# Router on rows ahead of their norm, and a top-k sorted in parts during the output projection

## The chip, the core and the metric

One core of one Trainium2 chip runs the whole program in one launch. The metric is device time in microseconds (us); less is better. Every time below comes from the recorded runs or from the profile of one execution.

## The reference, cut to what matters

One encoder layer on 1024 tokens of width 1024: an input norm and projection, three mixers (retention, S5, windowed attention), an output projection with a residual and a layer norm, and then sixteen SwiGLU experts, each of which takes the 128 tokens with the highest softmax affinity for it.

```
h   = LN(alpha*h + concat(retention, S5, attention) @ W_out)      # g = ln1_g, b = ln1_b
aff = softmax(h @ router_w)                                       # 1024 tokens x 16 experts
gates, idx = top_k(aff.T, 128)                                    # 128 tokens for each expert
xs  = h[idx]
out = (silu(xs @ w_gate) * (xs @ w_up)) @ w_down * gates          # for each expert
h   = LN(alpha*h + scatter_add(out))
```

## The kernel before

Tokens come in eight tiles of 128 rows (`NT`). The program has two halves.

**The mixers and the output projection.** A loop over `i` works in half tiles. A step computes the attention scores of one (tile, head group) pair, the attention output of the pair one step earlier (`attention_out`: DVE multiplies four score tiles by 1/sum in L790, PE transposes them into `tp`, ACT and DVE split them into a high and a low float32r part, PE multiplies with V), and one half of the output projection of a tile three steps behind that (`out_proj_half`, 24 matmuls of 512 columns, then `z = ALPHA*z + mm` on DVE, L838). After the second half, `out_proj_norm` does the layer norm (statistics on DVE, the power on POOL, L62 and L63 on DVE), stores the rows to `h1_dram` and ALPHA times the rows to `acc_dram`. Five steps later `router` transposes the normed rows, multiplies by `router_w` (L866, `rw` stationary, 128 columns moving), turns the 16 x 128 result back (L868, L870) and takes the softmax into `K.aff`. In this half a planner orders the instructions of each engine, from the order of the program, dependencies and its own cost estimates.

**The top-k.** `top_k` runs after all eight tiles: one transpose of the 128 x 128 affinities, eight rounds of maximum-of-8 and replace on two 64-column halves (L931, L934), bitonic merges (`bitonic`: two DVE instructions per stage, L886 and L887) on 128, 64 and 32 rows, a last merge over PE, the threshold `tau` (L956), masks, counting matmuls (L968 to L975) and `K.slot` (L984). `expert_hot`, `expert_slots` and `expert_gather` turn `slot` into token numbers; an indirect DMA on POOL gathers 128 rows of `h1_dram` (L1014).

**The experts.** 384 pieces of weights of 1 MB each pass through PE, 12 matmuls of 512 columns apiece. This half is ordered by hand on all engines. For each piece SP loads `wraw` (L1069), ACT copies the high part into `whl` (L71), DVE subtracts for the low part (L72). Eight raw buffers hold the first eight loads: two in pool `raw` (never closed), three in `raw2` (right end of the on-chip memory), three in `raw0`. Six `whl` buffers of 16 KB lie in `hl2` (left end). `Experts.start` issues the eight loads, six cuts (`cut` = high and low part; for pieces 0 to 2, `POOL_FIRST`, the low part is POOL's), and the first gather. The pools of the second half are opened where pools of the first half were closed, and the first use of a pool waits for all accesses of the closed pools whose bytes it takes: before, `raw2` lies over `hl` (which holds `rt`), `hl2` over `hy` (the output weights), `ast` and a part of `op` (the output projection's tiles).

Of the kernel before, what the change touches and what calls it, by code (L numbers as in the profile page):

```python
# [36 lines left out]
POOL_FIRST = 3  # L37
# [742 lines left out]
def attention_out(K, i):  # L780
# [8 lines left out]
    for g in range(4):  # L789
        nc.vector.tensor_scalar(S[g][:, :W], S[g][:, :W], rd[:, g:g + 1], None, op0=OP.mult)  # L790
# [28 lines left out]
def out_proj_load(K, t):  # L819
    nc, pool = K.nc, K.op  # L820
    y = pool.tile([P, 4, P], F32, name="y", bufs=2)
    nc.sync.dma_start(y, K.y_dram[t])
    z = pool.tile([P, D], F32, name="z", bufs=3)
    nc.sync.dma_start(z, K.h_dram[t])
    yh = pool.tile([P, KC, P], F32R, name="yh", bufs=3)
    yl = pool.tile([P, KC, P], F32R, name="yl", bufs=3)
    split(K, yh[:, 0:4, :], yl[:, 0:4, :], y)
    K.Y[t] = yh, yl, z


def out_proj_half(K, t, n):
# [6 lines left out]
    nc.vector.scalar_tensor_tensor(z[:, ns], z[:, ns], ALPHA, ps, op0=OP.mult, op1=OP.add)  # L838


def out_proj_norm(K, t):
    nc, pool = K.nc, K.op
    z = K.Y[t][2]
    layer_norm_tile(K, pool, z, z, K.g1, K.b1, "l1")
    nc.sync.dma_start(K.h1_dram[t * P:(t + 1) * P, :], z)
    K.rt[t] = K.hl.tile([P, 2, D], F32, name="rt", tag="whl")
    ah = K.rt[t][:, 0, :]
    nc.scalar.activation(ah, z, AF.Copy, scale=ALPHA)
    nc.sync.dma_start(K.acc_dram[t * P:(t + 1) * P, :], ah)


def router(K, t):
    nc, pool = K.nc, K.op
    z = K.Y.pop(t)[2]
    hT = K.rt.pop(t)[:, 1, :].rearrange("p (c f) -> p c f", c=KC)
# [11 lines left out]
    lT = pool.tile([E, P], F32, name="lT", bufs=2)  # L867
    nc.vector.tensor_copy(lT, pr[0:E, :])  # L868
    pl = K.psm.tile([P, E], F32, name="sm")
    nc.tensor.transpose(pl, lT, K.ident[0:E, 0:E])  # L870
    s = pool.tile([P, 4], F32, name="rsm", bufs=2)
    a = pool.tile([P, E], F32, name="aff", bufs=2)
    nc.vector.tensor_reduce(s[:, 0:1], pl, AX.X, OP.max)
    nc.vector.tensor_scalar(s[:, 1:2], s[:, 0:1], -1.0, None, op0=OP.mult)
    nc.scalar.activation(a, pl, AF.Exp, bias=s[:, 1:2], accum_out=s[:, 2:3])
    nc.vector.reciprocal(s[:, 3:4], s[:, 2:3])
    nc.vector.tensor_scalar(K.aff[:, t, :], a, s[:, 3:4], None, op0=OP.mult)


def bitonic(K, pool, x, rows, k, name):  # L880

    nc = K.nc
    while k:
        y = pool.tile([rows, P], F32, name=name, bufs=2)
# [24 lines left out]

def top_k(K):  # L910
# [4 lines left out]
    nc = K.nc  # L915
    aff = K.aff.rearrange("p t e -> p (t e)")
    with K.tc.tile_pool(name="topk", bufs=1, side="left") as pool:
        pt = K.ptp.tile([P, 4, P], F32, name="tp")
        nc.tensor.transpose(pt[:, 0, :], aff, K.ident)
        rest = [K.aff] + [pool.tile([P, NT, E], F32, name=f"rest{i}") for i in range(2)]  # L920
        for i in range(3):
            nc.gpsimd.tensor_copy(K.tok[:, :, :, 2 + i], rest[i])
            if i < 2:
                nc.gpsimd.tensor_tensor(rest[i + 1], rest[i], K.tok[:, :, :, 2 + i], OP.subtract)
        w = [[pool.tile([P, 64], F32, name=f"w{h}{i}") for i in range(2)] for h in range(2)]
        half = [pool.tile([P, 64], F32, name=f"half{h}") for h in range(2)]
        for h in range(2):
            nc.vector.tensor_copy(w[h][0], pt[:, 0, h * 64:(h + 1) * 64])
        for i in range(8):
            for h in range(2):  # L930
# [596 lines left out]
```

## Time and profile before

| what | value |
|---|---|
| median of three runs | 1745.15 us (1738.24, 1745.15, 1745.46) |
| the profiled execution's own time | 1739.56 us |
| its span, first to last instruction | 1737.9 us |
| busy: PE, DVE, ACT, POOL | 1608.6, 1435.3, 1058.7, 335.5 us |
| mean granted TensorE clock | 0.968 of full speed |
| read and written in the memory off chip | 465.01 MB, 46.14 MB |

The span is cut into stages by the lines that run in them. Busy time of an engine is a mean over stages with different limits, so the views of single stretches in the section on rows say more than this table.

### The profile page before, as it was taken

Reading aid. Unit: us, or ns where it says so; the run is one execution under the profiler, and the core shown is the slowest. Engines: PE = TensorE matmul, PEld = TensorE weight load, DVE = VectorE, ACT = ScalarE, POOL = GpSimd, SP = SyncE. Lnnn points to the kernel's source line nnn. Section 1 sums busy time; section 2 is a strip of 40 time slices with the busy share of each in tenths; the row PEclk is TensorE's granted clock in tenths of the full one; section 3 lists DMA queues with packets and bytes.
Section 4 is the critical chain, followed back from the end, with each engine's and each line's share of the span. In section 5 each row is a group of like instructions: output and inputs, shape, how many; then the busy total and the mean of one; then the engine's idle time right before and its main releaser. Section 6 shows DMA issues by size and latency. Waiting matters only on the chain.

```text
span 1737.9 us, 21027 instructions
## 1 busy us (share of the span) xinstructions
PE 1608.6 (93%) x7673; PEld 1294.0 (74%) x7673; DVE 1435.3 (83%) x1678; ACT 1058.7 (61%) x1082; POOL 335.5 (19%) x403
## 2 busy tenths in 40 slices
PE   6898996899993599999999999999999999999996
PEld 4688875577772488888888888888888778778785
DVE  8687962678867688888888889888898999989995
ACT  3332331455543377777777777777777777777772
POOL 6926801001003101011010010110101213121121
PEclk9999898999997699999999999999999999999998
DMA  6353189652225399999999999999999999999993
GB/s 246 115 143 102 51 244 267 196 176 74 77 105 242 113 337 370 371 387 356 382 377 370 383 362 376 382 371 383 366 372 409 384 396 412 382 406 376 394 402 138
DMA packets 110871, 512.53 MB, mean 295 GB/s; under 512 B 12336, under 2 KB 35120, under 8 KB 60080
## 3 DMA queue, kind: packets, MB, share of 16 engines
q1 hardware_dynamic: 100640, 481.31, 73.1%
q0 software_dynamic: 10128, 29.89, 5.6%
q8 instruction: 60, 0.98, 0.2%
q14 instruction: 43, 0.35, 0.1%
HBM read 465.01 MB, written 46.14 MB: 294 GB/s over the span
## 4 chain that ended last, share of the span: by engine, by line
PE 58%; DVE 14%; DMA 12%; issue 7%; ACT 4%; POOL 3%; SPq 1%; POOLq 0%; DVEq 0%; ACTq 0%
PE gu L1038 28%; PE y L1038 13%; DVE whl L72 5%; DMA zz<-acc_d 4%; PE mm L80 3%; PE mm L82 3%; PE mm L81 3%; ACT whl L71 2%; DMA wraw<-in_exp_w_down 2%; DMA wraw<-in_exp_w_up 2%; PE tp L1023 2%; PE tp L796 1%; PE sm L866 1%; PE po L81 1%; PE po L82 1%
## 5 line engine op out<-in xcount | busy, mean ns | idle before, releaser
L72 DVE TENSOR_TENSOR whl<-wraw,whl 128x2048 fp32r<-128x2048 f32 (+1 forms) x395 | 887.0, 2256 | 136.2 <-ACT whl L71 135.8
L71 ACT ACTIVATE whl<-wraw 128x2048 fp32r<-128x2048 f32 (+1 forms) x400 | 753.3, 1887 | 260.3 <-PE gu L1038 124.1
L1038 PE MATMUL gu<-whl,xT 128*128 128x512 f32 x3072 | 748.5, 400 | 0.0
L1038 PEld LDWEIGHTS gu<-whl,xT 128*128 128x128 f32 x3072 | 573.1, 189 | 130.7 <-ACT xT L71 0.3
L1038 PE MATMUL y<-whl,hT 128*128 128x512 f32 x1536 | 369.0, 396 | 0.7 <-ACT hT L71 0.7
L1038 PEld LDWEIGHTS y<-whl,hT 128*128 128x128 f32 x1536 | 288.6, 188 | 70.6 <-ACT hT L71 0.9
L1014 POOL DMA_INDIRECT xs<-h_d,index x16 | 44.8, 2798 | 755.9 <-issue 492.7
L80 PE MATMUL mm<-hT,whl 128*128 128x512 f32 x160 | 63.6, 398 | 6.2 <-DVE qst L75 5.3
L82 PE MATMUL mm<-hT,whl 128*128 128x512 f32 x160 | 63.1, 394 | 0.0
L81 PE MATMUL mm<-hT,whl 128*128 128x512 f32 x160 | 63.0, 393 | 0.0
L71 ACT ACTIVATE hT<-tp 128x512 fp32r<-128x512 f32 x80 | 46.4, 585 | 24.5 <-PE tp L141 15.4
L72 DVE TENSOR_TENSOR hT<-tp,hT 128x512 fp32r<-128x512 f32 x80 | 54.2, 681 | 7.1 <-ACT hT L71 7.1
L80 PE MATMUL mm<-WO,yh 128*128 128x512 f32 x128 | 51.2, 400 | 2.7 <-ACT yh L71 2.7
L80 PE MATMUL mm<-whl,hT 128*128 128x512 f32 (+1 forms) x128 | 47.3, 371 | 4.2 <-ACT gate L326 1.8
L81 PE MATMUL mm<-WO,yh 128*128 128x512 f32 x128 | 50.4, 393 | 0.0
L82 PE MATMUL mm<-WO,yl 128*128 128x512 f32 x128 | 50.1, 398 | 0.0
L1023 PE MATMUL tp<-ident,hid 128*128 128x128 f32 x256 | 38.8, 274 | 9.2 <-DVE hid L1122 9.1
L1023 PEld LDWEIGHTS tp<-ident,hid 128*128 128x128 f32 x256 | 31.2, 140 | 20.4 <-DVE hid L1122 12.6
L82 PE MATMUL mm<-whl,hT 128*128 128x512 f32 (+1 forms) x128 | 46.3, 363 | 0.0
L81 PE MATMUL mm<-whl,hT 128*128 128x512 f32 (+1 forms) x128 | 46.3, 364 | 0.0
L776 ACT ACTIVATE S<-S,asm 128x384 f32<-128x384 f32 (+1 forms) x64 | 36.9, 579 | 12.5 <-DVE asm L772 12.4
L1122 DVE TENSOR_TENSOR hid<-hid,gu 128x512 f32<-128x512 f32 x64 | 43.5, 679 | 0.0
(386 smaller groups left out, 1832.1 us busy)
## 6 DMA issues: line engine op xcount, KB each, us to landing
wraw<-in_exp_w_gate SPq DMA_DIRECT2D x128, 1024.0 KB, 7.4
wraw<-in_exp_w_up SPq DMA_DIRECT2D x128, 1024.0 KB, 7.2
wraw<-in_exp_w_down SPq DMA_DIRECT2D x128, 1024.0 KB, 8.0
wraw<-in_w_in SPq DMA_DIRECT2D x8, 1024.0 KB, 6.3
x<-in_x SPq DMA_DIRECT2D x8, 512.0 KB, 5.0
h_d<-x SPq DMA_DIRECT2D x8, 512.0 KB, 2.9
wraw<-in_w_out SPq DMA_DIRECT2D x4, 1024.0 KB, 5.7
q_d<-qst SPq DMA_DIRECT2D x64, 64.0 KB, 3.6
```

Source lines behind the costliest of these rows:

```text
L71: nc.scalar.activation(hi, src, AF.Copy)
L72: eng.tensor_tensor(lo, src, hi.bitcast(F32), OP.subtract)
L80: nc.tensor.matmul(ps, a[0], b[0], start=start, stop=False)
L81: nc.tensor.matmul(ps, a[0], b[1], start=False, stop=False)
L82: nc.tensor.matmul(ps, a[1], b[0], start=False, stop=stop)
L776: nc.scalar.activation(S[g][:, :W], S[g][:, :W], AF.Exp, bias=nm[:, g:g + 1], accum_out=rs[:, g:g + 1])
L796: nc.tensor.transpose(pt[:, g, :], S[g][:, (b - b0) * P:(b - b0 + 1) * P], K.ident)
L866: nc.tensor.matmul(pr[0:E, :], K.rw[:, c, :], hT[:, c, :], start=(c == 0), stop=(c == KC - 1))
L1014: nc.gpsimd.indirect_dma_start(out=xs, out_offset=None, in_=K.h1_dram, in_offset=bass.IndirectOffsetOnAxis(ap=K.index[:, e:e + 1], axis=0))
L1023: K.nc.tensor.transpose(pt[:, c, :], src[:, (c0 + c) * P:(c0 + c + 1) * P], K.ident)
L1038: nc.tensor.matmul(ps, a[s][c], u[:, t, i * w:(i + 1) * w], start=first and id(ps) not in began, stop=last and left[id(ps)] == 0)
L1122: at(self.after, q, 3, lambda: nc.vector.tensor_tensor(self.h[q], self.h[q], self.pg[q][1], OP.mult))
```

## The change

What it does, in the order of the program:

- `attention_out`: the four multiplications by 1/sum go from DVE to ACT. The buffers `yh` and `yl` go from three to two.
- The layer norm's gain g is multiplied into the router's weights once (`router_weights`; column sums of g*w and b*w by matmuls with ones). `router` transposes the rows `z` before they are normed; `affinities` corrects with mean, 1/deviation and the two sums. The product is now tokens x experts (`hT` stationary, 16 columns moving), so that the turning back is gone.
- `out_proj_norm` is cut into `out_proj_stats`, `out_proj_gain` and `out_proj_shift`. The lag from projection to router goes from five steps to one.
- The top-k is a generator run in chunks: tiles 0 to 3 are sorted while the projection goes on, then tiles 4 and 5 are merged in; tiles 6 and 7 remain for the end. For the last two tiles DVE's order is written by hand.
- Temporary tiles of the sort live in a pool `tk` on the left, between `ast` and `op`; those after the threshold in a pool `tks`, opened on the right after `hl` is closed and closed before `raw2` is opened.
- The count of tokens above the threshold is added by eight more matmuls of 128 columns; three DVE instructions form `slot` where eight did.
- In `Experts`, `cut` is split into `high` and `low`. `start` issues all six high parts, the gather, low parts 0 to 2 on DVE (not POOL), the first token tiles, then low parts 3 to 5. The gather is issued before the gate values are formed.

The diff, cut to its core:

```diff
@@ attention_out, out_proj_load
-        nc.vector.tensor_scalar(S[g][:, :W], S[g][:, :W], rd[:, g:g + 1], None, op0=OP.mult)
+        nc.scalar.activation(S[g][:, :W], S[g][:, :W], AF.Copy, scale=rd[:, g:g + 1])
-    yh = pool.tile([P, KC, P], F32R, name="yh", bufs=3)
+    yh = pool.tile([P, KC, P], F32R, name="yh", bufs=2)
@@ out_proj_half
+    nc.vector.bn_stats(K.st[t][:, n, :], z[:, ns])
@@ router
-    pr = K.psm.tile([P, P], F32, name="sm")
+    pr = K.psm.tile([P, E], F32, name="sm")
     for c in range(KC):
-        nc.tensor.matmul(pr[0:E, :], K.rw[:, c, :], hT[:, c, :], start=(c == 0), stop=(c == KC - 1))
+        nc.tensor.matmul(pr, hT[:, c, :], K.rw[:, 0, c, :], start=(c == 0), stop=(c == KC - 1))
...
+def affinities(K, t):
+    nc.vector.scalar_tensor_tensor(nl[:, 0], K.rsum[:, 0], mean, pr, op0=OP.mult, op1=OP.subtract)
+    nc.vector.scalar_tensor_tensor(nl[:, 1], nl[:, 0], rs, K.rsum[:, 1], op0=OP.mult, op1=OP.subtract)
+    nc.vector.tensor_reduce(s[:, 0:1], nl[:, 1], AX.X, OP.min)
+    if t == NT - 1:
+        out_proj_shift(K, t)
+    nc.scalar.activation(a, nl[:, 1], AF.Exp, scale=-1.0, bias=s[:, 0:1], accum_out=s[:, 1:2])
+    nc.vector.reciprocal(s[:, 2:3], s[:, 1:2])
...
+def sorted_rows(K, src, rows):            # 4 tiles, or 2 tiles doubled, on 128 partitions
+    for i in range(8):
+        nc.vector.max(half[0:2 * R, i * 8:i * 8 + 8], w[i % 2][0:2 * R])
+        if i < 7:
+            if i in (2, 5):
+                yield
+            nc.vector.match_replace(w[1 - i % 2][0:2 * R], half[0:2 * R, i * 8:i * 8 + 8], w[i % 2][0:2 * R], -1.0)
...
+    return (yield from bitonic(K, pool, both[0:R], R, 32, "bs"))
+
+def top_k_four(K):                        # tiles 0 to 3: sorted_rows, merged, merged_last
+def top_k_pair(K):                        # two tiles: sorted_rows, merged, maximum with K.best
+def top_k_two(K):                         # top_k_pair and seven more bitonic stages
@@ top_k
-        (one transpose, 8 rounds on two halves, bitonic on 128, 64 and 32 rows, a merge over PE)
+    m = yield from top_k_pair(K)
...
+    for t in range(NT):
+        nc.tensor.matmul(before[:, 1, :, :], K.order01[:, 1, :], g[:, 0, t:t + 1, :].to_broadcast([P, NT, E]),
+                         start=False, stop=(t == NT - 1))
+    for i in range(2):
+        nc.vector.scalar_tensor_tensor(w[:, i], before[:, i], -float(L), g[:, i], op0=OP.add, op1=OP.mult)
+    nc.vector.tensor_tensor(K.slot, w[:, 0], w[:, 1], OP.add)
@@ Experts.start
-        for k in range(POOL_FIRST):
-            self.cut(k)
+        for k in range(self.RING):
+            self.high(k)
         xs = expert_gather(K, 0, expert_slots(K, 0, expert_hot(K, 0)))
-        for k in range(POOL_FIRST, self.RING):
-            self.cut(k)
+        for k in range(3):
+            self.low(k)
         for half in range(2):
             self.tokens(0, xs, half, turned(K, xs, half * 4))
+        for k in range(3, self.RING):
+            self.low(k)
@@ build, the loop
+    for i in range(2 * NT + 1):
+        (scores, out_proj_load, attention_out as before)
+        next(sorts, None)
+        t, n = divmod(i - 5, 2)
+        if 0 <= t and n == 0:
+            if t == 5:
+                run(sorts)
+            router(K, t)
+            affinities(K, t)
+            out_proj_gain(K, t)
+            out_proj_shift(K, t)
+            if t in (3, 5):
+                sorts = top_k_four(K) if t == 3 else top_k_two(K)
+                next(sorts)
+        t, n = divmod(i - 3, 2)
+        if 0 <= t:
+            out_proj_half(K, t, n)
+            if n == 1:
+                out_proj_stats(K, t)
+            next(sorts, None)
+            next(sorts, None)
+    with tc.manual_schedule(engines={mybir.EngineType.DVE}):
+        t = NT - 1
+        router(K, t - 1)
+        next(sorts, None)
+        next(sorts, None)
+        affinities(K, t - 1)
+        run(sorts)
+        out_proj_gain(K, t - 1)
+        out_proj_shift(K, t - 1)
+        out_proj_half(K, t, 0)
+        out_proj_half(K, t, 1)
+        out_proj_stats(K, t)
+        router(K, t)
+        out_proj_gain(K, t)
+        affinities(K, t)
+        token_parts(K, 0, NT - 1)
+        token_parts(K, NT - 1, NT)
+        close(c_at2, c_hl)
+        c_tks, K.tks = pool("tks", side="right")
+        run(top_k(K))
+        close(c_tks)
+    close(c_op, c_tk, c_ast, c_s5s, c_hy)
```

## Rows read from the trace of the kernel before

**Rows 1.** Stretches: length, then each engine's busy us (instructions), TensorE clock, DMA share, GB/s.

```profile
core 0: us, PE busy (x) PEld busy (x) DVE busy (x) ACT busy (x) POOL busy (x), PEclk, DMA share, GB/s
...
500.00:520.00 20.00, 20.00 (x108) 15.09 (x107) 11.15 (x20) 6.56 (x12) 1.45 (x1) 1.00 0.23 77
...
540.00:560.00 20.00, 0.45 (x1) 0.18 (x1) 18.70 (x68) 11.35 (x8) 15.78 (x8) 0.52 0.98 409
...
760.00:800.00 40.00, 40.00 (x184) 32.43 (x183) 35.06 (x21) 29.45 (x21) 0.00 (x0) 1.00 0.99 386
...
455.00:527.00 72.00, 71.42 (x387) 54.70 (x387) 47.46 (x123) 32.34 (x79) 4.36 (x3) 1.00 0.24 84
```

**Rows 2.** The chain of waits, 520 to 640 us: start, length, what.

```profile
527.24 0.70 DVE z L838
...
533.40 1.94 PE sm L866 x16
...
540.83 0.46 PE tp L919
...
566.97 0.29 DVE tau L956
...
574.63 8.13 DMA xs<-h_d,index
...
584.78 10.32 PE gu L1038 x36
...
600.34 0.61 DVE hid L1122
...
620.00 0.44 PE tp L1023 x4
```

**Rows 3.** DVE in order of time, 546 to 600 us: start, length, what, idle before.

```profile
547.91 4.51 DVE L886 TENSOR_TENSOR b<-both 128x64 f32<-128x64 f32 x1
552.35 4.54 DVE L887 TENSOR_TENSOR b<-both 128x64 f32<-128x64 f32 x1
...
571.18 0.29 DVE L984 SCALAR_TENSOR_TENSOR slot<-sl 128x128 f32<-128x128 f32 x1
...
591.53 2.29 DVE L72 TENSOR_TENSOR whl<-wraw,whl 128x2048 fp32r<-128x2048 f32 x1 [4.19 <-ACT whl L71]
```

**Rows 4.** DVE instructions of the sort: count, ns least/median/most, first and last start.

```profile
L931 DVE MAX8 half<-w x16: 211/216/222, 541.6 to 546.3; 128x8 f32<-128x64 f32 x16
...
L934 DVE MATCH_REPLACE8 w<-half,w x14: 208/209/211, 541.9 to 546.0; 128x64 f32<-128x64 f32 x14
...
L886 DVE TENSOR_TENSOR b<-b x17: 212/217/227, 556.9 to 565.0; 64x64 f32<-64x64 f32 x6, 32x64 f32<-32x64 f32 x6, 128x64 f32<-128x64 f32 x5
```

**Rows 5.** POOL in order of time, 500 to 625 us.

```profile
529.23 1.45 POOL L61 TENSOR_TENSOR l1rs<-l1rs,mhalf 128x1 f32<-128x1 f32 x1 [14.58 <-DVE l1rs L60]
...
543.03 4.53 POOL L72 TENSOR_TENSOR whl<-wraw,whl 128x2048 fp32r<-128x2048 f32 x1
...
547.82 8.98 POOL L72 TENSOR_TENSOR whl<-wraw,whl 128x2048 fp32r<-128x2048 f32 x2
```

**Rows 6.** SP's DMA queue in order of time, 520 to 640 us.

```profile
538.83 0.81 SPq L1069 DMA_DIRECT2D wraw<-in_exp_w_up  x2
```

**Rows 7.** ACT in order of time, 500 to 625 us.

```profile
540.92 7.31 ACT L71 ACTIVATE whl<-wraw 128x2048 fp32r<-128x2048 f32 x4 [0.70 <-DVE aff L877]
548.68 1.91 ACT L71 ACTIVATE whl<-wraw 128x2048 fp32r<-128x2048 f32 x1 [0.45 <-DMA wraw<-in_exp_w_gate]
551.16 1.91 ACT L71 ACTIVATE whl<-wraw 128x2048 fp32r<-128x2048 f32 x1 [0.57 <-DMA wraw<-in_exp_w_gate]
```

**Rows 8.** The sixteen gathers into xs: us from issue to landing.

```profile
DMA to landing us min/median/max: 8.1/10.5/12.5
```

**Rows 9.** Groups by line and shape, 340 to 541 us: busy us, mean ns, idle before.

```profile
L776 ACT ACTIVATE S<-S,asm 128x384 f32<-128x384 f32 x48 | 29.0, 606 | 11.6 <-DVE asm L772 11.6
...
L790 DVE TENSOR_SCALAR S<-S,asm 128x384 f32<-128x384 f32 x48 | 17.1, 412 | 0.2
```

More of the change, by code (lines that the diff above doesn't have):

```diff
@@ L880, in bitonic, with run @@
+def run(gen):
+    for _ in gen:
+        pass
 def bitonic(K, pool, x, rows, k, name):
@@ L883, in bitonic @@
     while k:
-        y = pool.tile([rows, P], F32, name=name, bufs=2)
+        if k in (16, 2):
+            yield
+        y = pool.tile([64, P], F32, name=name, tag="b", bufs=2)[0:rows]
         a, b = (v.rearrange("p (n two k) -> p n two k", two=2, k=k) for v in (x, y))
@@ new lines, in merged, with merged_last @@
+def merged(K, x):
+    nc, pool = K.nc, K.tk
+    o = pool.tile([32, P], F32, name="om", tag="om")
+    nc.vector.tensor_copy(o, x[32:64, ::-1])
+    m = pool.tile([64, P], F32, name="mm", tag="m", bufs=2)[0:32]
+    nc.vector.tensor_tensor(m, x[0:32], o, OP.max)
+    return (yield from bitonic(K, pool, m, 32, 64, "bm"))
+def merged_last(K, x):
+    nc, pool = K.nc, K.tk
+    rev = pool.tile([32, P], F32, name="om")
+    nc.vector.tensor_copy(rev, x[:, ::-1])
+    pt = K.ptp.tile([P, 4, P], F32, name="tp")
+    nc.tensor.transpose(pt[:, 0, 0:32], x, K.ident[0:32, 0:32])
+    nc.tensor.transpose(pt[:, 1, 0:32], rev, K.ident[0:32, 0:32])
+    m = pool.tile([P, 2, E], F32, name="mh")
+    nc.vector.tensor_copy(m[:, 0, :], pt[:, 0, 0:E])
+    nc.vector.tensor_tensor(m[:, 1, :], m[:, 0, :], pt[:, 1, E:2 * E], OP.max)
+    pt = K.ptp.tile([P, 4, P], F32, name="tp")
+    nc.tensor.transpose(pt[0:E, 0, :], m[:, 1, :], K.ident)
+    x = pool.tile([64, P], F32, name="ml", tag="m", bufs=2)[0:E]
+    nc.vector.tensor_copy(x, pt[0:E, 0, :])
+    return (yield from bitonic(K, pool, x, E, 64, "bl"))
@@ new lines, in top_k_four @@
+def top_k_four(K):
+    twice = K.tk.tile([P, 2, 4, E], F32, name="twice")
+    K.nc.scalar.activation(twice, K.aff[:, None, 0:4, :].to_broadcast([P, 2, 4, E]), AF.Copy)
+    top = yield from sorted_rows(K, twice.rearrange("p a t e -> p (a t e)"), 64)
+    top = yield from merged(K, top)
+    top = yield from merged_last(K, top)
+    K.best = K.tk.tile([E, P], F32, name="best", bufs=2)
+    K.nc.vector.tensor_copy(K.best, top)
+def top_k_pair(K):
+    top = yield from sorted_rows(K, K.pair.rearrange("p a t b e -> p (a t b e)"), 64)
+    top = yield from merged(K, top)
+    m = K.tk.tile([64, P], F32, name="mt", tag="m", bufs=2)[0:E]
+    K.nc.vector.tensor_tensor(m, K.best, top[0:E, ::-1], OP.max)
+    return m
@@ L1170, in quarter @@
                 fn()
-            self.cut(self.taken + self.RING)
+            self.high(self.taken + self.RING)
+            self.low(self.taken + self.RING)
             self.taken += 1
@@ L1409, in build @@
         pass
+    c_tk, K.tk = pool("tk")
     c_op, K.op = pool("op")
```

225 lines of the change are left out of this document (111 added, 114 removed).

## The prediction

> **What bounds the kernel now.** I read the slices of the page first, then the windows, then the chain of waits. The windows [rows 1] show two stretches in which PE never rests: the output projection (20.00 of 20 us busy at 500 to 520) and the experts (40.00 of 40 at 760 to 800, clock 1.00). Between them lies a hole: from 540 to 560 PE is busy 0.45 us and its granted clock is 0.52, about the lower of its two levels, while DVE works 18.70 us. The chain [rows 2] walks through the hole. The last half of the projection is summed at 527.24, the top-k begins with a transpose at 540.83, the gather is issued at 574.63, and the first expert matmul starts at 584.78: 57.5 us from the projection's last sum to the experts. Since PE sets the pace on both sides, what the hole loses the kernel gains, less what PE must do or wait for extra elsewhere.
>
> DVE's own list [rows 3] shows that not all of the hole is sorting: two instructions of the first bitonic stage take 4.51 and 4.54 us, while seventeen others of the same line take 0.217 at the median [rows 4]. POOL at that time subtracts the low parts of the first weights, 4.53 us each, 8.98 us for the last two [rows 5]: the first slow DVE instruction ends where the first of these two would, the second at the end of both (556.8). Some 8.6 us of the top-k are a wait for POOL.
>
> **The change part by part.** All sums go against the profiled execution (1739.56 us; span 1737.9). It lies 5.6 below the median of the three runs, 1745.15.
>
> *From the last sum to the top-k, 13.6 us before* (527.24 to 540.83). The rows now go to PE without waiting for power and norm. I add up: sum 0.7, statistics 1.1, copy of the second transposed half 0.7 on DVE; half of the router's matmuls behind it, about 1.0 of the 1.94 that sixteen take [rows 2]; the multiplication by g hides under them. Then two corrections and the minimum 0.65, the shift 1.3 (ACT's exponential hides under it), reciprocal, scaling and the way to PE 0.75. With gaps, 6.5 us. Saved: 7.1.
>
> *The top-k, 30.6 us before* (540.83 to the end of `slot`, 571.18 + 0.29 = 571.47 = S). Two tiles remain, doubled on 128 partitions. One chain of rounds in place of two interleaved: maximum 0.216 and replace 0.208 [rows 4], with value load and gaps 0.55 a round as a dependent chain, 4.1 for eight. Stages of bitonic cost 0.39 a pair; 6 + 7 of them are 5.0. Transpose, copies, reversals, the maximum with the four-tile result: 2.3. That is 11.4 to the threshold. From threshold to `slot` it was 4.5 (566.97 to 571.47): five DVE instructions fewer, but eight matmuls of 128 columns more at the lower clock, so I keep 4.4. Sum 15.8; saved 14.8, of which 8.6 are the wait for POOL and the rest is sorting moved away.
>
> *What the removed work becomes.* The six low parts on DVE take 2.29 us each [rows 3]. The first three run while the gather is under way, as three did before. The last three now stand behind the token tiles, where DVE had 4.19 us free before the low part at 591.53. They need 6.9, which pushes the chain of that list (next hot mask, low parts 6 to 8, product of gate and up) about 0.6 beyond 600.34, and PE waits for that product. Loss 0.6.
>
> *The weights behind the new pool.* The eight loads fill `raw`, `raw2` and `raw0`. Before, the third load was issued at 538.83 [rows 6], when the last reader of `hl` had finished, with 46 us to go. Now `tks` occupies the right end between `hl` and `raw2`, and its last reader is the instruction that writes `slot`. SP issues in order, so loads three to eight cannot start before S. Likewise `hl2` now lies over `tk`, so the first high part must wait for the threshold instead of 540.92 [rows 7]; those two ACT copies still fit before S. In the old run the third of the six loads landed 9.8 us after the first issue (548.6) and the next 2.5 later (551.1) [rows 6, 7]. Piece 5, the last needed for the six high parts, is the fourth of them: S + 0.4 + 12.3, plus 1.25 for the gather's half MB on the same engines, is S + 14.0. Its high part (1.91) and the token tile behind it on ACT (0.6) give S + 16.5 for the first expert matmul; before it was 584.78 - S = 13.3. The gather itself took 8.1 us on quiet engines (the first) and 10.5 at the median beside loads [rows 8], which lands it at S + 13 and so earlier than piece 5; issuing it 0.3 earlier gains nothing. Loss 3.2; from 0 (if the loads get through earlier than I think) to 6 (gather at its longest, 12.5, and its transposes behind).
>
> *PE in the projection.* Routers 5 and 6 now stand before the last projection half, one transposing and two multiplying more. Sixteen router instructions took 1.94 [rows 2]; four transposes, each with its own 128-column weights, 0.44, so sixteen such weight loads are at most 1.76, and no row speaks against half of that. I take 1.4 a router. The turning back (0.3 each, my estimate from a transpose in rows 2 and its hand-over) is gone, the sort adds six small transposes, the weight sums some 32 short matmuls early on, where PE has gaps. Together the last sum comes 2 later (from -2 to +4).
>
> *DVE and ACT in the projection.* The sort of four tiles is 16.1 us by the same prices (11.1 plus the merge over PE, 5), that of the next two 14.3: 30.4 us on DVE. In the 72 us from 455 to 527 DVE was busy 47.46 [rows 1]. It loses some twenty multiplications of 0.412 [rows 9], 8 us, and gains 28 net of waits for PE: 67 or 68 of 72. It just fits; bursts will not. PE waits for DVE's low parts of `pT` and `yl`. ACT takes the multiplications at about the 0.606 of its exponential on the same tile [rows 9], and was busy 32 of 72, so it has room. I take 2 us of waiting (0 to 10, by how much of the sort comes in bursts).
>
> **Sum.** -7.1 - 14.8 + 0.6 + 3.2 + 2 + 2 = -14.1: 1725.5 against the profiled execution, 1731.0 against the median. I forecast 1728, between the two.
>
> **The lock between POOL and DVE.** The slow pair of rows 3 shows a DVE instruction with both inputs on chip held for a whole POOL instruction. That bears on the change too: every `merged` and bitonic step in the projection is of that kind, and POOL's power of each tile reads the same memory, 1.45 us [rows 5]. Tiles 4 to 7 fall into sorting time, so at most 4 x 1.45 = 5.8 us of DVE are lost, and if all reach PE the time is 1731.3. Against it: that power at 529.23 seems itself stretched by the multiplication before it. The Trainium skill, SBUF — State Buffer, section "Who interferes with whom", states the rule: a VectorE instruction with two SBUF inputs contends with a GpSimd instruction that reads SBUF, and the loser blocks for the whole instruction. By that rule the 8.6 us come back in full, and the trace agrees (4.51 against 0.217).
>
> **Rivals.** *A, DVE overruns in the projection.* The four-tile sort comes in three chunks per step over steps 11 to 13, some 31 us in which DVE already works two thirds of the time (47.46 of 72) [rows 1], so 16 more overfill it by 5. For it: PE has no reserve there (71.42 of 72). Against it: scores are computed ahead, so DVE may fall behind some steps before PE runs dry, and after the scores its load is 11.15 of 20. If 10 us reach PE the gain falls to 6 (1733.5, no measurable change). If all 30.4 do, the last sum comes 28 later than in my sum and the time is 1753.9, slower. The point between is 16 us of exposed sorting.
>
> *B, the weights starve PE at the restart.* If the six loads run slower than 2.5 us each because gather and stores are among them, or pieces 6 to 10 come late too, the loss at S is 9 and not 3.2: 1731.3, within 0.5%. For it: no load can be ahead of S. Against it: PE takes more than 2.8 us for a piece of twelve matmuls at the restart (36 in 10.32) [rows 2], and a load came every 2.5.
>
> *C, the change does not do what it says.* The planner may leave the chunks for the end, since nothing but the last two tiles needs them; DVE's hand-written tail then runs all that is left before the last sums. If the two-tile sort (14.3) stands there whole, PE's last tile of 11 us covers a good part and 7 remain: 1732.5. If the four-tile sort is there too, 1748.
>
> **How the numbers follow.** About 0.5% (8.7 us) is what a measurement of this kernel can tell from no change. Forecast, a gain of 9 to 23: 0.72. A: 0.11 without measurable change, 0.04 slower. B: 0.06. C: 0.04 same and 0.01 slower. The lock at its worst: 0.02. So faster 0.72, same 0.23, slower 0.05. Low end: PE 2 earlier, no waits, no late weights, -23.3 from 1739.56, 1716. High end: the losses of A and B partly together, against the median, 1740; beyond it lies about one in ten.
>
> **What would show it.** Right: no DVE bitonic instruction over 1 us after the projection; about 6.5 us from the last L838 sum to the pair's transpose and about 16 from there to `slot`; the third weight load issued at the end of `slot`, the first expert matmul about 16.5 later. Wrong: PE idle by more than 5 us between 440 and 530; sort instructions crowded before the last sum; PE waiting for `whl` in the first ten pieces.

## The result and the profile after

| what | before | after |
|---|---|---|
| median of the ten runs of the comparison | 1740.56 us | 1754.58 us |
| ratio, 95% interval | | 1.0075 [1.0055, 1.0095] |
| profiled execution: own time, span | 1739.56, 1737.9 us | 1756.48, 1754.7 us |
| mean granted TensorE clock | 0.968 | 0.961 |

The kernel became 0.75% slower, some 13 us. The forecast was 1728 us, in a range of 1716 to 1740; the measured time lies above it.

The windows of after, with the columns of [rows 1]:

```profile
455.00:527.00 72.00, 64.88 (x337) 50.42 (x336) 52.26 (x180) 40.26 (x100) 1.68 (x3) 0.95 0.16 57
...
485.00:490.00 5.00, 4.54 (x16) 3.52 (x17) 3.64 (x16) 1.00 (x2) 0.00 (x0) 0.50 0.00 0
...
455.00:545.00 90.00, 82.18 (x430) 64.29 (x428) 66.11 (x241) 44.92 (x109) 2.21 (x4) 0.96 0.16 57
```

In [rows 1] PE worked 71.42 of the 72 us from 455 to 527 at clock 1.00. Now it works 64.88, and from 485 to 490 the granted clock is 0.50, the lower of the two levels. DVE is busy 52.26 us there, and still PE waits. This isn't the 67 or 68 that I worked out, but my sum had put both sorts into this window, and that of tiles 4 and 5 comes behind it; up to 545 DVE is busy 66.11 of 90. Where PE waits, its timeline says (start, length, what, idle before):

```profile
482.68 0.33 PE L984 MATMUL tp<-ident,twice 128*128 128x128 f32 x1 [3.08 <-ACT twice L1034]
482.85 0.60 PE L795 MATMUL tp<-ident,S 128*128 128x128 f32 x4
...
507.35 0.21 PE L1019 MATMUL tp<-ident,bm 32*128 32x32 f32 x1 [0.73 <-DVE bm L947]
...
508.32 0.27 PE L1025 MATMUL tp<-ident,mh 128*16 128x128 f32 x1 [0.56 <-DVE mh L1023]
...
513.70 0.66 PE L795 MATMUL tp<-ident,S 128*128 128x128 f32 x4 [0.89 <-DVE pT L71]
...
544.87 0.40 PE L81 MATMUL mm<-WO,yl 128*128 128x512 f32 x1
554.34 1.11 PE L883 MATMUL tp<-ident,z 128*128 128x128 f32 x4 [9.07 <-DVE z L837]
```

The sort's own small transposes (`twice`, `bm`, `mh`) now stand in PE's order between attention and projection, and PE is idle at each until the engine ahead of it is done. That work behind such a transpose waits with it, the first of them shows: the attention transposes at 482.85 are, by the order of the pairs, those of the scores that ACT had multiplied from 465.37 to 467.51, and yet they begin only behind it. The waits of 0.89 us and the like for `pT` are attention's own, for low parts that DVE makes with sort instructions ahead of them. The last projection matmul starts at 544.87 (before: 526.81), and the transpose of the sum comes 9.07 us of idle PE later. DVE's timeline shows what it did in that time:

```profile
531.85 0.26 DVE L913 TENSOR_SCALAR pair<-aff,rsm 128x64 f32<-128x64 f32 x1
533.49 0.46 DVE L988 COPY w<-tp 64x64 f32<-64x64 f32 x2 [1.38 <-PE tp L984]
...
550.89 0.21 DVE L1056 COPY best<-bo 16x128 f32<-16x128 f32 x1
551.04 1.27 DVE L920 SCALAR_TENSOR_TENSOR z<-z,l1mv,g 128x1024 f32<-128x1024 f32 x1
552.34 1.34 DVE L927 SCALAR_TENSOR_TENSOR z<-z,l1rs,b 128x1024 f32<-128x1024 f32 x1
553.61 0.67 DVE L837 SCALAR_TENSOR_TENSOR z<-z,mm 128x512 f32<-128x512 f32 x1
...
554.93 0.67 DVE L837 SCALAR_TENSOR_TENSOR z<-z,mm 128x512 f32<-128x512 f32 x1
```

The affinities of tiles 4 and 5 are complete only at 531.85. Their sort runs from 533.49 to 551.04, and both last sums stand behind it in DVE's order, with gain and shift of tile 6 (551.04 and 552.34). The last sum starts at 554.93 where it was 527.24 [rows 2], 27.7 us later.

The hole itself went as forecast. Chain of waits, after (start, length, what):

```profile
562.51 0.46 PE tp L984
...
578.57 0.30 DVE slot L1089
...
578.94 0.33 SPq L1174
...
580.34 12.22 DMA wraw<-in_exp_w_gate
592.58 1.91 ACT whl L1180
```

From the last sum to the top-k it is 7.6 us, the top-k takes 16.4 (562.51 to 578.87), and from there to the first expert matmul (595.02) it is 16.2. No bitonic instruction after the projection takes over 0.3 us.

**A common zero.** The four matmuls that end the stage before (`mm<-yT`) start at 339.37 in the profile of before, and at 336.7 to 342.9 in those of the other kernels, though nothing ahead of them was edited. Positions of one profile against another are therefore given from this start ("from zero") in the table, which holds the study; S is the end of `slot`. "Tile 4" is the start of the second sum of tile 4, a second mark, which lies ahead of the first sort chunk in every kernel that sorts early.

| kernel (zero at) | tile 4 | last projection matmul | last sum | top-k begins | S | ratio to before |
|---|---|---|---|---|---|---|
| before (339.37) | 123.6 | 187.4 | 187.9 | 201.5 | 232.1 | 1 |
| e1_lows (338.62) | 125.0 | 188.8 | 189.2 | 204.5 | 225.3 | 0.9944 [0.9919, 0.9968] |
| e2_two_buffers (338.69) | 120.0 | 189.4 | 189.8 | 203.4 | 234.0 | 1.0012 [0.9984, 1.0040] |
| e3_act_multiply (342.85) | 122.3 | 190.8 | 191.2 | 206.1 | 236.8 | 1.0032 [1.0013, 1.0052] |
| e12_wide_and_late (337.63) | 133.8 | 189.6 | 190.0 | 205.8 | 227.2 | 0.9956 [0.9940, 0.9973] |
| e10_late_routers (336.72) | 134.9 | 190.6 | 191.1 | 206.8 | 228.2 | 0.9989 [0.9967, 1.0012] |
| e9_wide_sums (338.07) | 132.1 | 191.3 | 192.5 | 199.9 | 221.4 | 0.9937 [0.9917, 0.9957] |
| e5_rows_and_lows (339.68) | 135.0 | 194.1 | 195.3 | 201.9 | 223.4 | 0.9990 [0.9975, 1.0006] |
| e4_no_early_sort (337.05) | 135.6 | 197.1 | 198.2 | 205.4 | 226.8 | 0.9954 [0.9932, 0.9975] |
| e11_no_pair_sort (337.25) | 135.3 | 206.7 | 207.9 | 215.3 | 231.7 | 1.0023 [1.0007, 1.0038] |
| after (337.85) | 132.3 | 207.0 | 217.1 | 224.7 | 241.0 | 1.0075 [1.0055, 1.0095] |
| e6_pool_left (338.45) | 133.7 | 208.9 | 219.0 | 226.6 | 242.8 | 1.0072 [1.0044, 1.0100] |
| e7_sums_first (337.58) | 135.6 | 210.3 | 210.8 | 224.4 | 240.8 | 1.0066 [1.0041, 1.0090] |
| e13_routers_first (336.76) | 133.1 | 203.3 | 213.4 | 221.0 | 237.3 | 1.0051 [1.0031, 1.0070] |
| e14_mended (339.21) | 129.9 | 197.9 | 208.0 | 215.5 | 231.7 | 0.9998 [0.9978, 1.0018] |
| e15_late_routers_2 (338.72) | 133.3 | 189.0 | 189.5 | 200.4 | 226.4 | 0.9977 [0.9959, 0.9995] |
| e8_sort_later (337.55) | 134.7 | 203.7 | 213.3 | 220.9 | 237.2 | 1.0050 [1.0028, 1.0073] |

Two readings of the table carry what follows. First, before, e1, e2 and e3 order PE's work otherwise and can't be compared with the rest at tile 4. Among the rest, e4, e6, e7, e8, e11 and after have the same code up to there, and still differ by up to 3.3 us. Most of it is idle time of PE ahead of the weight sums, some 20 us from zero, for which the profile shows no cause: none in after, 1.09 us in e6, 1.40 in e11, 2.00 in e8, 2.55 in e7, 3.41 in e4. Behind tile 4 the profiles repeat well: to the last projection matmul it is 55.75 us in e10, e12 and e15 alike, and 74.7 in after and in e7. So what the sort costs is better read from tile 4 than from zero.

Second, the positions account for the times. Against before, the first expert matmul comes 10.7 us earlier (e9) to 11.9 later (after) from zero, and in fifteen of the sixteen kernels this lies within the interval of the ratio. The exception is e5: 8.8 earlier in its profile, but 1.7 faster by its ratio (from 4.4 faster to 1.0 slower). Its profiled run, 1732.95 us, is among its fastest; the median is 1737.47. Why is open.

### The profile page after: what moved, and what is told of

Same layout as the page of the kernel before. It is cut to its first block, busy times and chain, and to the rows that moved or that the text cites. A ratio compares the mean times of both kernels' runs of the same rounds, so it can differ in the third digit from the quotient of the medians.

```text
span 1754.7 us, 21200 instructions
## 1 busy us (share of the span) xinstructions
PE 1622.7 (92%) x7699; PEld 1311.8 (75%) x7699; DVE 1433.0 (82%) x1721; ACT 1092.5 (62%) x1151; POOL 323.2 (18%) x406
## 4 chain that ended last, share of the span: by engine, by line
PE 54%; DVE 16%; DMA 12%; issue 7%; ACT 6%; POOL 3%; SPq 1%; POOLq 0%; DVEq 0%; ACTq 0%
PE gu L1143 26%; PE y L1143 13%; DVE whl L1187 5%; DMA zz<-acc_d 4%; PE mm L79 3%; PE mm L81 3%; PE mm L80 3%; DMA wraw<-in_exp_w_down 3%; ACT whl L1180 2%; PE tp L1128 2%; DMA wraw<-in_exp_w_up 1%; DMA wraw<-in_exp_w_gate 1%; PE tp L795 1%; DMA q_d<-qst 1%; PE sm L890 1%
## 5 line engine op out<-in xcount | busy, mean ns | idle before, releaser
L1187 DVE TENSOR_TENSOR whl<-wraw,whl 128x2048 fp32r<-128x2048 f32 x384 | 874.5, 2289 | 121.4 <-ACT whl L1180 121.0
L1180 ACT ACTIVATE whl<-wraw 128x2048 fp32r<-128x2048 f32 x384 | 736.8, 1922 | 280.9 <-PE gu L1143 125.4
L70 ACT ACTIVATE hT<-tp 128x512 fp32r<-128x512 f32 x80 | 46.5, 585 | 25.9 <-PE tp L140 15.7
L79 PE MATMUL mm<-whl,hT 128*128 128x512 f32 (+1 forms) x128 | 48.4, 379 | 4.2 <-ACT gate L325 1.8
L81 PE MATMUL mm<-whl,hT 128*128 128x512 f32 (+1 forms) x128 | 47.8, 375 | 0.6 <-DVE hT L71 0.6
L80 PE MATMUL mm<-whl,hT 128*128 128x512 f32 (+1 forms) x128 | 47.4, 373 | 0.1
L70 ACT ACTIVATE pT<-tp 128x512 fp32r<-128x512 f32 x44 | 25.6, 591 | 29.4 <-PE tp L795 29.2
```

Of the source, the lines that this page charges most:

```text
L70: nc.scalar.activation(hi, src, AF.Copy)
L79: nc.tensor.matmul(ps, a[0], b[0], start=start, stop=False)
L80: nc.tensor.matmul(ps, a[0], b[1], start=False, stop=False)
L81: nc.tensor.matmul(ps, a[1], b[0], start=False, stop=stop)
L1180: self.K.nc.scalar.activation(u[:, 0, :], self.raw[k].rearrange("p a b -> p (a b)"), AF.Copy)
L1187: self.K.nc.vector.tensor_tensor(u[:, 1, :], raw, u[:, 0, :].bitcast(F32), OP.subtract)
```

## The experiments

**Parts of the change on the kernel before.** e1 takes only the hand order of the experts' start: all high parts, gather, low parts 0 to 2 on DVE, and low parts 3 to 5 behind the token tiles.

```diff
-        for k in range(POOL_FIRST):
-            self.cut(k)
+        for k in range(self.RING):
+            self.high(k)
         xs = expert_gather(K, 0, expert_slots(K, 0, expert_hot(K, 0)))
...
+        for k in range(3):
+            self.low(k)
...
+        for k in range(3, self.RING):
+            self.low(k)
```

> The kernel before with one part alone: the six high parts first, then the gather (issued before the gate values), low parts 0 to 2 on DVE and not on POOL, low parts 3 to 5 behind the token tiles. If the two slow DVE instructions of the first bitonic stage are a wait for POOL, none of that line takes more than 0.3 us, the top-k falls from 30.6 to about 22 us, and the whole time by about 8 (9.4 less 0.6 to 1.5 for the later low parts): 1732. If they are slow for a reason of their own, nothing changes (within 3 us).

1734.69 against 1741.62 us: faster, by 0.56%. The first stage of bitonic on DVE's timeline, in e1:

```profile
549.01 0.22 DVE L885 TENSOR_TENSOR b<-both 128x64 f32<-128x64 f32 x1
549.15 0.22 DVE L886 TENSOR_TENSOR b<-both 128x64 f32<-128x64 f32 x1
```

The 4.51 and 4.54 us of [rows 3] are 0.22, and the top-k takes 20.9 us where it took 30.6. The wait for POOL was real, and its removal needs nothing else of the change.

e2 has two buffers of `yh` and `yl` for three, e3 the multiplication by 1/sum on ACT.

```diff
-    yh = pool.tile([P, KC, P], F32R, name="yh", bufs=3)
-    yl = pool.tile([P, KC, P], F32R, name="yl", bufs=3)
+    yh = pool.tile([P, KC, P], F32R, name="yh", bufs=2)
+    yl = pool.tile([P, KC, P], F32R, name="yl", bufs=2)
```

> The kernel before with yh and yl of two buffers in place of three, nothing else. Theory 1 (the sort delays the last projection sum by some 28 us, the rest of the change by little): the last sum stays within 2 us of 527.2 and the time within 3 us. Theory 2 (the other parts of the loop cost it): the last sum comes 5 or more later.

1743.82 us, a ratio that can't be told from no change (0.9984 to 1.0040). The last sum is 1.3 later in the profile, as theory 1 has it, and 1.9 from zero.

```diff
-        nc.vector.tensor_scalar(S[g][:, :W], S[g][:, :W], rd[:, g:g + 1], None, op0=OP.mult)
+        nc.scalar.activation(S[g][:, :W], S[g][:, :W], AF.Copy, scale=rd[:, g:g + 1])
```

> The kernel before with the four multiplications by 1/sum on ACT in place of DVE, nothing else. Theory 1: last sum within 2 us of 527.2. Theory 2: ACT's longer chain (four times 0.53 in place of 0.41) keeps PE waiting and the last sum comes 5 or more later.

1747.62 us, slower by 0.32%. The last sum is 6.8 later in its profile, theory 2's mark; but 3.5 of it had been lost before zero, ahead of the edit, so 3.3 are left, between the theories. The multiplication on ACT isn't free; that two buffers cost something is not shown.

**The change with parts taken out.** e4 is after with the whole old top-k at the end and no early sort; e5 is e4 with the multiplication on DVE and three buffers.

```diff
@@ e4, on after; `top_k` itself is the old one
...
-            if t in (3, 5):
-                sorts = top_k_four(K) if t == 3 else top_k_two(K)
-                next(sorts)
...
-        run(top_k(K))
+        top_k(K)
```

> The changed kernel with the whole top-k at the end, as in the kernel before (all eight tiles, the old code), and with nothing sorted during the projection; router on raw rows, two buffers, multiplication on ACT, weights' order all as changed. Theory 1: the last sum comes at 527 + 5 = 532 (routers 5 and 6 and the weight sums before it), not at 554.9; from there 7.5 to the top-k, about 22 for it, 13.5 to the first expert matmul: 575 against 584.8 before, a whole time 9 to 10 below the kernel before. Theory 2: the last sum comes at 540 or later and the time is not below the kernel before.

1735.82 us: without the early sort the rest of the change is faster than before, though no more so than e1 alone. The last sum, 535.27, lies between the marks of the two theories. From zero it comes 18.9 earlier than in after (22.1 from tile 4), and the top-k, the old one, takes 21.4 us.

> Router on raw rows and the weights' order as changed; the whole top-k at the end as before, and, unlike the run without early sorting, the multiplication by 1/sum back on DVE and three buffers for yh and yl. If the multiplication on ACT (6.8 us in its own run) and the two buffers (1.3) make up the 8 us that the last sum was late without any sort, it now comes at 527 to 530, the first expert matmul at 570, and the time is 13 to 15 below the kernel before (1727). If the early router itself holds PE up, the last sum stays at 533 or later and the time at 1735.

1737.47 against 1739.75 us, no faster than before within the interval and a miss: the last sum (534.98) is still 7.4 later than before from zero. Something else of the change, with no sort and no ACT multiplication, holds PE. By its ratio e5 is also slower than e4, though its S is 3.5 earlier from zero: this is the exception named under the table. e9 and e10 look for it.

```diff
@@ e9, on e5: router_weights
-    ps = K.psm.tile([P, 2, E], F32, name="sm")
+    ps = K.psm.tile([P, 2, KC, E], F32, name="sm")
...
-        for c in range(KC):
-            nc.tensor.matmul(ps[:, i, :], ones, K.rw[:, i, c, :], start=(c == 0), stop=(c == KC - 1))
+    nc.tensor.matmul(ps, ones, K.rw, start=True, stop=True)
...
-    nc.vector.tensor_copy(K.rsum, ps)
+    nc.vector.tensor_reduce(K.rsum, ps.rearrange("p i c e -> p i e c"), AX.X, OP.add)
```

> Rows-ahead router and new weight order without early sort (as in e5), but the sums of the router's weights over the model dimension are made by one matmul of 256 columns and a DVE sum, where 32 matmuls of 16 columns took 3.4 to 3.9 us of PE. Theory 1 (PE has no reserve before the last projection, so every us of work put ahead of it delays it by a us): last projection sum 2.5 to 3.5 earlier than in e5 (534.98), the top-k's transpose too, time 1735. Theory 2 (those matmuls lie where PE waits anyway): within 1 us of e5.

1731.44 us against 1741.10, the fastest of the study by its median, with e1 within the intervals. PE's timeline, e5:

```profile
361.87 3.64 PE L869 MATMUL sm<-rwg,ones 128*128 128x16 f32 x32
```

and e9:

```profile
361.40 0.98 PE L868 MATMUL sm<-rwg,ones 128*128 128x256 f32 x2
```

The last sum is 2.8 earlier from zero: theory 1, what PE does 170 us ahead of the end moves the end. Tile 4 is summed 2.9 earlier already, and from there on e5 and e9 agree within 0.1. The time fell by more than these 2.8 us; of the two ratios e5's is the one that its positions don't bear out.

```diff
@@ e10, on e5: the loop
-        if 0 <= t and n == 0:
+        if 0 <= t < 5 and n == 0:
...
-        router(K, t - 1)
...
-        affinities(K, t - 1)
...
-        out_proj_gain(K, t - 1)
-        out_proj_shift(K, t - 1)
         out_proj_half(K, t, 0)
         out_proj_half(K, t, 1)
         out_proj_stats(K, t)
+        for u in (t - 2, t - 1):
+            router(K, u)
+            affinities(K, u)
+            out_proj_gain(K, u)
+            out_proj_shift(K, u)
```

> As e5, but the routers of tiles 5 and 6 stand behind the last projection half, where the kernel before had those of its last tiles. Theory 1 (a router is 2.4 to 2.5 us of PE wherever it stands; early routers only move PE work from behind the last sum to ahead of it): last sum 5 earlier than in e5, about 530; the time from it to the top-k's transpose grows from 6.6 to 10 or 11, and the transpose stays within 2 us of 541.6, the time within 3 us of e5. Theory 2 (the early router itself, by its shorter chain, is what brings the top-k forward): the transpose comes 4 or more later than in e5.

1739.78 us. The last sum came at 527.77, the transpose of the top-k at 543.53: by these positions theory 1. From zero the transpose is 4.9 later than in e5 (5.0 from tile 4), which is theory 2, and 15.8 us lie between sum and transpose where 10 or 11 were expected. The trace of e10 says why it can't decide: PE waits 2.00 and 2.86 us there for DVE, which does gain and shift of tiles 5 and 6 in that place. e15 moves these behind the last affinities.

```diff
@@ e15, on e10
         for u in (t - 2, t - 1):
             router(K, u)
             affinities(K, u)
-            out_proj_gain(K, u)
-            out_proj_shift(K, u)
         router(K, t)
         out_proj_gain(K, t)
         affinities(K, t)
+        for u in (t - 2, t - 1):
+            out_proj_gain(K, u)
+            out_proj_shift(K, u)
```

> As e10 (routers of tiles 5 and 6 behind the last projection half), with gain and shift of these tiles behind the last affinities, so that PE doesn't wait for DVE between the routers. Theory 1 (an early router only moves PE work from behind the last sum to ahead of it): transpose of the top-k 4 to 5 earlier than in e10, within 1 us of e5's 201.9 us after the stage's start. Theory 2 (the early router brings the top-k forward by itself): 2 us or less earlier than in e10 (206.8).

1735.78 us. From zero the transpose comes 6.4 earlier than in e10 and 1.5 earlier than in e5; from tile 4 it is 4.8 earlier than in e10 and within 0.2 of e5, which are theory 1's marks. But S is 3.0 later than in e5 (4.7 from tile 4): the four multiplications of gain and shift, 1.28 to 1.49 each, now stand in the top-k, 25.9 us instead of 21.4. So the early router's own work is PE work moved from behind the last sum to ahead of it; what it gains is that DVE's gain and shift find cover.

e12 joins e9's and e10's edits.

> Both edits of e9 and e10 on e5. If they add: last sum at about 527, transpose of the top-k at 538 to 540, first expert product 3 us earlier than in e5 (592.0), time 1731 to 1735, a little below e1 at best. If the planner's order moves more than the edits do: anywhere within 3 us of e5.

1735.10 us. The last sum, 527.63, came where expected, but the transpose, 543.40, missed the 538 to 540: it waits as in e10. The wide sums moved the last sum by 1.1 from zero here and not by 2.8, all of it ahead of tile 4. In this order the two edits don't add.

**The early sort, priced by itself.** e11 leaves out the sort of tiles 4 and 5, whose affinities then never enter its top-k.

```diff
-                sorts = top_k_four(K) if t == 3 else top_k_two(K)
-                next(sorts)
+                sorts = top_k_four(K) if t == 3 else iter(())
+                next(sorts, None)
```

> The changed kernel without the sort of tiles 4 and 5 (left out altogether: their affinities never enter the top-k, all else stays). Theory 1 (the last two sums wait for that sort in DVE's queue, and PE's end is set by the four-tile sort): last projection matmul at 544 as before or 1 to 3 earlier, last sum within 1 us of that and so 9 to 13 earlier (542 to 546), top-k's transpose 9 to 12 earlier, time 1744 or less. Theory 2 (PE's end too is delayed by the pair): last projection matmul 5 or more earlier, last sum 538 or less. Theory 3 (the tail is bound by router and affinities of tiles 6 and 7): last sum less than 4 earlier.

1744.98 us; theory 1, but for 1 us of its time. DVE's timeline in e11, the two last sums:

```profile
543.77 0.68 DVE L837 SCALAR_TENSOR_TENSOR z<-z,mm 128x512 f32<-128x512 f32 x1
...
545.10 0.67 DVE L837 SCALAR_TENSOR_TENSOR z<-z,mm 128x512 f32<-128x512 f32 x1
```

PE's last matmul is at 543.99, 0.9 earlier than in after, the last sum 9.8 earlier (0.3 and 9.2 from zero). So the pair costs the 9 us of DVE's tail, and the four-tile sort, in e11 but not in e4, costs PE 9.7 from zero (206.7 against 197.1). From tile 4 the four-tile sort costs 10.0, and the pair 12.2: 3.3 on PE and 8.9 in DVE's tail.

**Mends of the change.** e6 opens `tks` on the left, so that the weight loads needn't wait for `slot`.

```diff
-        c_tks, K.tks = pool("tks", side="right")
+        c_tks, K.tks = pool("tks")
```

> The changed kernel with the pool tks opened on the left, behind op, so that raw2 takes none of its bytes. If the third weight load waits for slot because of these bytes, it is issued some 15 us before slot, and the first expert matmul follows slot by about 13.3 us in place of 16.2: a time 2.5 to 3 below the changed kernel. If the loads were not what the restart waited for, 16.2 stays.

1749.88 us. The third load was issued 12.5 us before S and the first expert matmul came at S + 13.2, as before the change, not S + 16.2. So the load behind `tks` cost 3.0. The time can't show it: from zero the last sum came 1.9 later, 1.4 of it ahead of tile 4, and the interval, 1.0044 to 1.0100, is wider than the gain.

e7 puts the last two sums ahead of the rest of the sort in DVE's tail.

```diff
@@ e7, on after
         router(K, t - 1)
-        next(sorts, None)
-        next(sorts, None)
         affinities(K, t - 1)
-        run(sorts)
-        out_proj_gain(K, t - 1)
-        out_proj_shift(K, t - 1)
         out_proj_half(K, t, 0)
...
         router(K, t)
+        run(sorts)
+        out_proj_gain(K, t - 1)
+        out_proj_shift(K, t - 1)
```

> The changed kernel with one order changed in DVE's hand-written tail: the two sums of the last tile, its statistics and the router's copies stand ahead of what is left of the four-and-two sort. If the last sum waits in DVE's queue behind that sort, it now follows PE's last projection matmul within 2 us (8 to 9 earlier), and the rest of the sort fills the wait for the router's product: the last top-k starts 4 to 6 earlier, the time is 4 to 6 below the changed kernel. If PE and not the queue sets it, nothing moves.

1750.42 us, no better than after. The last sum now follows PE's last matmul within 0.5 us. From zero it came 6.3 earlier, the top-k 0.2; but 3.2 us had been lost ahead of tile 4, before anything that was edited. From tile 4 the last sum is 9.5 earlier and the top-k 3.5, a little under the 4 to 6 expected: the order of DVE's tail gives back 3.5 of the 12.2 that the pair costs there, and the time doesn't show even that. e8 begins the four-tile sort one step later (three calls of `next` pass ahead of its first chunk).

> The changed kernel with the sort of the first four tiles begun one step later in the program, so that its operand is ready before PE reaches the transpose. If PE's 3.1 us wait in its queue and the lower clock after it (10 us at 0.5 to 0.9) cost what they seem to, the last projection matmul comes 4 to 6 earlier and the time falls by as much. If the sort's load on DVE is what holds PE up, wherever it stands, it moves by less than 2.

1748.03 us; last matmul 3.3, last sum and top-k 3.8 earlier from zero, between the two marks. From tile 4 it is 5.7 for the matmul, within the 4 to 6 expected, and 6.1 for the others. PE's timeline in e8 has the sort's first transpose without a wait:

```profile
485.80 0.27 PE L990 MATMUL tp<-ident,twice 128*128 128x128 f32 x1
```

The granted clock stays at 1.00 from 475 to 500. So the place of the first chunks, with the wait of 3.08 and the lower clock behind it, costs that much.

e13 gives the routers and affinities of tiles 0 to 5 the first place in the planner's order; e14 adds the edits of e6 and e9.

```diff
-            router(K, t)
-            affinities(K, t)
+            with tc.high_priority():
+                router(K, t)
+                affinities(K, t)
```

> The changed kernel, with router and affinities of tiles 0 to 5 put first in the planner's order. In the profile of the changed kernel tile 5 is summed at 499.9, but its transposes come at 518.9 and 523.9 and its affinities at 531.9, 13 us ahead of the last projection matmul; the sort of the pair takes 17.5 us. Theory 1 (the sort of tiles 4 and 5 is exposed because the planner lets the router wait): affinities of tile 5 by 512, the pair sorted before PE's last matmul, last sum within 2 us of that matmul, so 7 to 9 us earlier than 554.9, time 1746. Theory 2 (DVE's queue before that is full, or PE stops more often for the earlier sort): the pair's sort moves forward, but the last matmul moves back by as much or more, time within 3 us of 1754.6.

1749.13 us, and neither theory. Tile 5's affinities came at 526.84, 5.0 earlier (3.9 from zero), but PE's last matmul too (540.10, 4.8 earlier, 3.7 from zero), so the cover stayed 13.3 us and the last sum moved along, to 550.13. Priority did not take the router to its sum: from tile 5's sum (493.35) to its affinities it still took 33.5 us.

> As e13, with the sums of the router's weights as one wide matmul (e9) and the weight loads freed from the wait for slot (e6). If the early sort can be made to pay by such mends: last sum at 542 or less, S at 566 or less, first expert matmul at S + 13.2, time 1740, and so still above e9 (1731). Below 1731 it would show that sorting early pays; above 1748 that the mends don't add.

1740.15 us, level with before. The last sum, 547.16, and S, 570.95, came some 5 us later than expected, the first expert matmul at S + 13.2. The mends give back the loss and no more: e9, without any early sort, is some 9 us faster.

## Why the prediction was wrong

**The step that failed.** It is the pair "PE in the projection" (2) and "DVE and ACT in the projection" (2): I had priced the two at 4 us; the last sum came 27.7 later, 29.2 from zero. The table, read along kernels that differ by a part, gives a ledger from 187.9 to 217.1. Its last column is what of it lies behind tile 4:

| part | last sum later by | behind tile 4 |
|---|---|---|
| rows ahead of the norm, order of weights (before to e12) | 2.1 | not comparable |
| routers of tiles 5 and 6 ahead of the last half (e12 to e9) | 2.5 | 4.2 |
| sums of the weights in 32 short matmuls (e9 to e5) | 2.8 | under 0.1 |
| multiplication on ACT, two buffers (e5 to e4) | 2.9 | 2.3 |
| sort of tiles 0 to 3 (e4 to e11) | 9.6 | 9.9 |
| sort of tiles 4 and 5 (e11 to after) | 9.2 | 12.2 |

So the early sort makes up 18.8 of the 29.2, and 22.1 if what PE lost ahead of tile 4 is left out. The parts are sizes within this order only: e12 shows that they don't simply add, and each kernel is planned anew. The first row also holds something that no run priced by itself: in the changed loop the projection trails attention by two steps and not three (`i - 3`).

*PE.* I wrote that the weight sums fall "early on, where PE has gaps". They took 3.64 us in e5; the wide form saves 2.66, and 2.8 reached the last sum (1.1 in the order of e10 and e12). The product with 16 columns I priced at about half of 1.76; sixteen take some 1.6 us, and with the transposes a router is 2.4 where I took 1.4. Two routers ahead of the last half cost 4.2 behind tile 4.

*DVE and ACT.* I summed DVE's busy time (67 of 72: "it just fits") and priced only what bursts would cost. By busy time DVE did fit, 66.11 us of the 90 from 455 to 545. What didn't fit was the order: the sort is a chain that passes through PE, and the work behind a waiting link waits too. The first wait, 3.08, is for an ACT copy behind the four multiplications that the change gave to ACT (480.30, 2.13 us in one run). The seven waits of PE from 480 to 516 for DVE or that copy add up to 6.5 us. Behind the first, from 485 to 490, PE works 4.54 us at a granted clock of 0.50, by my estimate a loss of 2.3, and some 0.7 more at 480 to 485 and 490 to 495 (clock 0.92, 0.89). From tile 4 to the last matmul after takes 74.7 us and e4 61.4. Of these 13.3 us the waits and the clock are 9.5, less 0.7 for e4's one wait in the stretch; the rest, later waits of 0.9 and PE's work for the sort's transposes among it, I did not price. e8, which has neither the first wait nor the lower clock, got back 5.7 of it.

*The end of the sort.* Under A I took a late sort to be covered by scores computed ahead, under C the pair by "PE's last tile of 11 us". But the pair can't begin before tile 5's affinities, and these are done at 531.85, 13.0 us ahead of PE's last matmul; 17.5 us of sorting, with other work of DVE between, don't fit. I had read the lag of one step in the program as one step in time. (It went to one from four: the five that I gave count from the first half of a tile's projection, the one from the second.) Tile 5 was summed at 499.88: its affinities trailed by 32 us, and in e4 and e5, without a sort, by 26.

**What held.** Measured against the prediction: last sum to top-k 7.6 (6.5), top-k 16.4 (15.8), S to the first expert matmul 16.2 (16.5), third load at the end of `slot` (so forecast), product of gate and up at S + 31.8 where before it was at S + 28.8 (3.8 later forecast: 0.6 and 3.2). Each of these sizes was right within about a us, and e1 and e6 show the mechanisms of two, POOL's lock and the load behind `tks`. Of the signs of being wrong, two came: PE was idle 7.1 us between 440 and 530, and sort instructions stood crowded before the last sum.

**The gain that was left.** From the start of the top-k to S the change saves 14.2 us, but 9.7 of them are e1's, the lock. Against e4's old top-k without the lock (21.4), sorting six tiles early saves 5.1 (16.4). It costs 18.8 at the last sum. That is the verdict on this part.

**The sum again.** From zero S comes 8.9 later; the time from S to the first expert matmul is 3.0 longer. Together 11.9, against 13 of the ratio (9.6 to 16.5 by its interval).

**The rivals.** A came out in time and place (1753.9 us if all of the sort reached PE, against 1754.58), with 0.04 for its slower case. But its mechanism, DVE filled to more than its time, isn't what the trace shows: about 19 of 30 us were exposed (22 from tile 4), by PE's order and by DVE's tail, and PE's extra work made up the rest. That A's number came out is luck. C's tail, the pair ahead of the last sums, did happen, with 9.2 exposed for the 7 that I worked out, though not because the planner left the chunks lying. B fell: ACT's waits for the loads put their landings 2.3 to 3.5 us apart, with the gather among them, and piece 5 landed at S + 13.7 (14.0 forecast). The lock over POOL's power in the tail cost nothing that could be seen: the power takes 0.54 or 0.55 us in after in place of the 1.45 of [rows 5]. For the pair of [rows 3], e1 (0.22 us for 4.51) bears out what the Trainium skill says in SBUF — State Buffer, section "Who interferes with whom": the loser waits for the whole of the other's instruction.

**What stays open.** Why the affinities of tiles 0 to 5 trail their tile's sum by 26 to 45 us in every kernel with the new lag, sort or not, was not found; priority took off 5 us at the most (for tile 4, 45.2 in after and 39.9 in e13) and nothing for tile 5 (33.5 in e13). If they came at once, the pair would have cover; no run tried that by another means. Open too are the idle time of PE ahead of the weight sums and the ratio of e5.

## What to carry to other kernels

When work moves under a busy engine, sum the free time of the engine that does it, but then follow the moved chain instruction by instruction: every hop over the busy engine is a place where it can stop, with all the work behind it, and the last piece can begin only when its data exist, so the time from there to the end of the cover is the cover. Price each part of a change against the change without it: the order of the weights, a few lines, gave all the gain that can be told from noise, and the largest part gave 5 us for 19. And when two profiles are compared, set a mark close ahead of what was edited, and count from there.

## What the runs showed of the hardware

- Short matmuls aren't short: 32 of 128x16 in float32 took 3.64 us, about 0.11 each, while one product with 256 columns of the same values (two instructions) took 0.98, in a stretch whose granted clock was 0.70 (361 to 363 in e9).
- A wait of 3.08 us of PE was followed by 5 us at a granted clock of 0.50 (the 1.2 GHz level), though PE worked 4.54 of them: by my estimate the stop cost some 2.3 us beyond itself.
- POOL's power of 128x1 takes 0.54 us by itself. It is still 1.45 in e1, where DVE's order around it is that of before, so that the 1.45 of [rows 5] is probably the other side of the lock. After shows the same: POOL's first subtraction of 128x112, begun at 551.08 just behind DVE's multiplication at 551.04, took 1.52 us; its second, at 554.12, took 0.44.
